# Where a transposed order is made: in TensorE's moving operand, or where ACT and DVE take the results over

## The chip, the cores and the metric

One NeuronCore of one Trainium2 chip. The metric is the device time of one execution in microseconds; the median of three runs of the kernel before is 582.38 us (581.98 to 582.94).

## The reference

An encoder layer on 512 tokens of 1024 channels, all float32. The tokens form a grid of 8 rows by 64 columns.

```python
h = rms_norm(x, g_pre) * (1.0 + scl) + shift
xa, za, q, k, v, zb, ga, gb = split(h @ w_in)          # each 512 x 1024
y_a = (rg_lru(conv(xa), forward) + rg_lru(conv(xa), backward)) * silu(za)
y_a = y_a @ w_pa
y_b = neighbourhood_attention(q, k, v, rpb) * silu(zb)  # 16 heads of 64, 8 rows x 16 columns of keys
y_b = y_b @ w_pb
merged = sigmoid(ga) * y_a + sigmoid(gb) * y_b
out = rms_norm(x + gate * (merged @ w_o), g_final)
```

## The kernel before

All activations are kept transposed: channels on the partitions, the 512 tokens along the free axis. A projection (`proj`) makes 128 output channels: it runs over eight blocks of 128 input channels, and for each issues three matmuls (`mm3`) of 128 x 128 weights against 128 x 512 tokens, since every float32 operand is split into a high and a low part of type fp32r (`whi` and `wlo` for weights, `hh`/`hl` or `hhl` for h, `ybhl` for y_b). That is 24 matmuls into one PSUM bank of the class `acc`.

The attention works on blocks of columns: the 64 columns of the grid are four blocks of 16, and all queries of one block (8 rows x 16 columns, 128 queries) share one window of 24 or 32 columns of keys. It therefore wants q, and everything that comes out of it, in the order *block, row, column*, while h, k and all of the rest are in the order of the tokens, *row, block, column*. In the kernel before the order is changed by TensorE as it reads its moving operand. The view `tok` takes 16 floats, hops 64 floats to the next row, and starts again 16 floats on for the next block:

```python
tok = lambda t: t.rearrange("p (r b c) -> p b r c", b=4, c=16)
nat = lambda t: t.rearrange("p (b r c) -> p r b c", b=4, c=16)
hhq, hlq = ([(d[k], lambda t=d[k]: tok(t.ap)) for k in range(KD)] for d in (hh, hl))
```

The projections of q and of zb (called z, the gate of the attention) read h through `tok`, so their results come out in block order. The projection of y_b with `w_pb` reads `ybhl`, which is in block order, through `nat` (16 floats, hop of 128), so its result comes out in token order. All other projections read plain tiles.

The main part runs in this order. First v is made (PSUM class `hx`), then eight rounds for eight pairs of heads: `proj` for q, k and z, and `attention(pr, q, k, z, ...)`. Then four groups of eight projections: two xa (`conv_gates`, with small matmuls into `gt`), two za (`gate_a`), two gates (`gate_m`), two of y_b with `w_pb`; then gates and `w_pa` in turn, and last the product with `w_o`.

In `attention`, ACT makes `qh` (L686) and `kh`, DVE the remainders `ql` (L687) and `kl` (helper, L339); the scale -1/8 is applied to q. Scores (`sp`) are twelve matmuls for two blocks; DVE adds the bias and takes the minimum (L717), ACT makes the exponential (L723), TensorE transposes (`pt`, L732), ACT and DVE split the result (`pp`, L737 and L739), TensorE multiplies with v (`pv`), ACT and DVE add the parts into `yt` (L754 to L760). The sums' reciprocals are spread (`rcx`, L775) and transposed into a bank `rcb` (L780, tile class `mi`); DVE multiplies the gate `sz` by 0.5 and by it (`szr`, L782), then `yt` by `sz` (`yb`, L784), and ACT and DVE split the product into `ybhl` (L336, L339).

The order of instructions on every engine is set by a planner (`Plan`) that simulates costs and ranks, so an attention's scores, transposes and products with v are interleaved with the projections that follow: the second half of a pair's attention lies beside the q and k of the next pair, and the eighth pair's beside the first xa projections. Weight tiles are cast by ACT (`whi`, L336) and split by DVE or POOL (`wlo`, L339); their loads are issued by SP and held back by the progress of TensorE (`gate_of`).

Of the kernel before, what the change touches and what calls it, by code (L numbers as in the profile page):

```python
# [8 lines left out]
F32 = mybir.dt.float32  # L9
F32R = mybir.dt.float32r  # L10
AF = mybir.ActivationFunctionType
ALU = mybir.AluOpType

P = 128
S = 512
D = 1024
KD = D // P
# [51 lines left out]
class Plan:  # L69
# [18 lines left out]
    def op(self, eng, cost, fn, rank, r=(), w=(), rw=(), lock=False, after=(), spare=0, size=0, until=None, name=""):  # L88
        o = Op()
        o.alts = {eng: cost} if isinstance(eng, str) else dict(zip(eng, cost))  # L90
        o.fn, o.rank, o.lock, o.spare, o.size, o.name = fn, rank, lock, spare, size, name
        o.n, o.until = len(self.ops), until
        deps = set()
        for t in list(r) + list(rw):
            for f in t.family():
                deps.update(f.writers)
        for t in list(w) + list(rw):
            for f in t.family():
                deps.update(f.readers)
        for t in r:  # L100
            t.readers.append(o)
        for t in w:
            t.writers.append(o)
        for t in rw:
            for f in [t] + t.parts:
                f.writers, f.readers = [], []
            t.writers = [o]
        o.tiles = list(dict.fromkeys(t.base or t for t in list(w) + list(rw) + list(r)))
        for t in o.tiles:
            t.uses += 1  # L110
        o.data, o.succ, o.t = set(deps), [], 0.0
        deps.update(after)
        o.left = len(deps)
        for d in deps:
            d.succ.append(o)
        self.ops.append(o)
        return o
# [155 lines left out]
def act(n, ptr=0, acc=False):  # L273
    return 0.19 + 0.833e-3 * n + 0.093 * ptr + 0.19 * acc


def dve(n):
    return 0.153 + 1.043e-3 * n
# [6 lines left out]
def pool_(n):  # L285
    return 0.17 + 2.33e-3 * n


def pe(n, passes=1):
    return passes * max(n / 2400.0 + 0.0135, 0.111)  # L290
# [3 lines left out]
def layer(ctx, tc, x, par, w_m, w_g, bc_gate, w_v, w_in, w_blk, rpb, amask, w_pa, w_pb, w_o, g_final, out):  # L294
    nc = tc.nc
# [6 lines left out]
    op = pl.op  # L302
# [6 lines left out]
    def T(name, dt=F32):  # L309
        return pl.tile("s", lambda i: sb.tile([P, S], dt, tag=f"s{i}", name=nm(name)))  # L310

    def W(name, dt=F32):
        return pl.tile("w", lambda i: sb.tile([P, D], dt, tag=f"w{i}", name=nm(name)))

    def two(name):

        t = W(name, F32R)
        return t.part(0, S), t.part(S, D)

    def B(cls):  # L320
        return pl.tile(cls, lambda i: ps.tile([P, 512], F32, tag=f"b{i}", name=nm(cls)))
# [7 lines left out]
    def load(t, dst, src, rank, size, after=(), spare=0, r=(), name="load"):  # L329

        return op("SP", 0.45, lambda e: nc.sync.dma_start(dst(), src() if callable(src) else src), rank,  # L331
                  r=r, w=[t], after=after, spare=spare, size=size, name=name)

    def cast(o, i):

        return lambda e: nc.scalar.copy(o(), i()) if e == "ACT" else nc.vector.tensor_copy(o(), i())  # L336

    def sub(o, a, b):
        return lambda e: ENGINE[e].tensor_tensor(o(), a(), b().bitcast(F32), op=ALU.subtract)  # L339
# [4 lines left out]
    def mm3(o, lh, ll, rh, rl, first, last):  # L344
        mm(o, lh, rh, first, False)
        mm(o, lh, rl, False, False)
        mm(o, ll, rh, False, last)

    def whole(t):
        return lambda: t.ap  # L350


    def const(name, shape, dt=F32):
# [14 lines left out]
       r=[par_sb, ident], w=[pp0])  # L368
# [62 lines left out]
    for t in range(NT):  # L431
# [7 lines left out]
        if t % 2:  # L439
            rstd_ops(2, [qap[i], qdp[i]], lambda i=i: (qa.ap[:, 2 * i:2 * i + 2], qd.ap[:, 2 * i:2 * i + 2]), -16.8 + 2 * i, rx[i])  # L440
            for h in range(2):
                for u in (t - 1, t):
                    def scale(e, u=u, h=h, i=i):
# [6 lines left out]
                       lock=True)  # L450
# [27 lines left out]
    hh, hl = {}, {}  # L478
# [134 lines left out]
    def gate_of(n, back):  # L613
        return [main[max(0, n - back)]] if n - back >= 0 else []

    def proj(w, rh, rl, lo="DVE"):

        n = len(main)
        raw, hi, low = W("wraw"), W("whi", F32R), W("wlo", F32R)
        v = lambda t: (lambda: t.ap.rearrange("p (k c) -> p k c", k=KD))  # L620
        load(raw, whole(raw), w, n - 5, 524288, after=gate_of(n, 5), spare=1,
             name=f"w{n}")
        op("ACT", act(1024), cast(whole(hi), whole(raw)), n - 2.2, r=[raw], w=[hi], after=gate_of(n, 3), name=f"whi{n}")
        engs = (lo,) if isinstance(lo, str) else lo
        costs = [dve(1024) if e == "DVE" else pool_(1024) for e in engs]
        op(engs, costs, sub(whole(low), whole(raw), whole(hi)), n - 2.1, r=[raw, hi], w=[low], lock=True, name=f"wlo{n}")
        o = B("acc")
        for k in range(KD):
            def f(e, k=k):
                mm3(o.ap, v(hi)()[:, k, :], v(low)()[:, k, :], rh[k][1](), rl[k][1](), k == 0, k == KD - 1)  # L630
            first = op("PE", pe(512, 3), f, 1000 + n + 0.01 * k, r=[hi, low, rh[k][0], rl[k][0]], rw=[o], name=f"p{n}")
            if k == 0:
                main.append(first)
        return n, o
# [2 lines left out]
    H = (slice(0, 64), slice(64, 128))  # L637

    tok = lambda t: t.rearrange("p (r b c) -> p b r c", b=4, c=16)
    nat = lambda t: t.rearrange("p (b r c) -> p r b c", b=4, c=16)  # L640
    hhl, hll = ([(d[k], whole(d[k])) for k in range(KD)] for d in (hh, hl))
    hhq, hlq = ([(d[k], lambda t=d[k]: tok(t.ap)) for k in range(KD)] for d in (hh, hl))

    def bias(pr, rank, after):
        raw = T("braw")
# [33 lines left out]
    ybh, ybl = {}, {}  # L679

    def attention(pr, q, k, z, nbt, pos):

        nq, oq = q
        nk_, ok = k
        qh, ql, kh, kl = (T(n, F32R) for n in ("qh", "ql", "kh", "kl"))
        op("ACT", act(512), lambda e: nc.scalar.activation(qh.ap, oq.ap, AF.Copy, scale=-0.125), nq - 1.9, r=[oq], w=[qh], name="qh")  # L686
        op("DVE", dve(512), lambda e: nc.vector.scalar_tensor_tensor(ql.ap, oq.ap, -0.125, qh.ap.bitcast(F32), op0=ALU.mult,  # L687
           op1=ALU.subtract), nq - 1.9, r=[oq, qh], w=[ql], name="ql")
        op("ACT", act(512), cast(whole(kh), whole(ok)), nk_ - 1.9, r=[ok], w=[kh], name="kh")
        op("DVE", dve(512), sub(whole(kl), whole(ok), whole(kh)), nk_ - 1.9, r=[ok, kh], w=[kl], name="kl")  # L690
        sm, yt = C("sm", 8), T("yt")
        off = (pr % 2) * 256
        def half(b0):
# [73 lines left out]
        sz, rc, rcb = T("sz"), C("rc", 8), B("mi")  # L767
# [4 lines left out]


        rx_ = T("rcx")
        op("ACT", act(512), lambda e: nc.scalar.copy(rx_.ap.rearrange("p (b c) -> p b c", b=8),  # L775
           rc.ap.unsqueeze(2).to_broadcast([P, 8, 64])), pos - 0.3, r=[rc], w=[rx_], name="rcx")

        def f(e_):
            for b in range(4):
                nc.tensor.transpose(rcb.ap[:, b * P:(b + 1) * P], rx_.ap[:, b * P:(b + 1) * P], ident.ap)  # L780
        op("PE", 0.47, f, pos - 0.3, r=[rx_, ident], w=[rcb], name="rcb")
        op("DVE", dve(512), lambda e: nc.vector.scalar_tensor_tensor(sz.ap, sz.ap, 0.5, rcb.ap, op0=ALU.mult, op1=ALU.mult),  # L782
           pos - 0.3, r=[rcb], rw=[sz], name="szr")
        op("DVE", dve(512), lambda e: nc.vector.tensor_tensor(yt.ap, yt.ap, sz.ap, op=ALU.mult), pos + 0.5, r=[sz], rw=[yt],  # L784
           lock=True, name="yb")
        ybh[pr], ybl[pr] = two("ybhl")
        op("ACT", act(512), cast(whole(ybh[pr]), whole(yt)), pos + 0.6, r=[yt], w=[ybh[pr]], name="ybh")
        op("DVE", dve(512), sub(whole(ybl[pr]), whole(yt), whole(ybh[pr])), pos + 0.6, r=[yt, ybh[pr]], w=[ybl[pr]], lock=True,
           name="ybl")

    def small(rank, after):
# [32 lines left out]
    LO_A = ("POOL",)  # L824
    att = []
    for pr in range(8):
        n0 = len(main)
        nbt = bias(pr, n0, gate_of(n0, 2) if pr else [main[6]])
        if pr % 2 == 0:
            load_v(pr // 2, gate_of(n0, 2) if pr else [])  # L830
        q = proj(w_in[16 + pr], hhq, hlq, LO_A if pr else "DVE")
        k = proj(w_in[24 + pr], hhl, hll, LO_A)
        z = proj(w_in[32 + pr], hhq, hlq, LO_A)
        attention(pr, q, k, z, nbt, k[0] + 0.6)


# [112 lines left out]
    for g in range(4):  # L949
        tiles = (2 * g, 2 * g + 1)  # L950
        n0 = len(main)
        ybv = lambda: ([(ybh[k], lambda t=ybh[k]: nat(t.ap)) for k in range(KD)], [(ybl[k], lambda t=ybl[k]: nat(t.ap)) for k in range(KD)])
        load_gates(g, n0, gate_of(n0, 3))
        for i in tiles:
            conv_gates(i, proj(w_in[i], hhl, hll))
        for i in tiles:
            gate_a(i, proj(w_in[8 + i], hhl, hll))
        recur(tiles, n0 + 10)
        for i in tiles:
            gate_m((i, 0), proj(w_in[48 + i], hhl, hll))  # L960
        for i in tiles:
            prod_m((i, 0), proj(w_pb[i], *ybv()), None)
# [128 lines left out]
    pos = [B("acc") for _ in range(NT)]  # L1091
# [8 lines left out]
    for t in range(NT):  # L1100
        for h in range(1 + (t == NT - 1)):
            w = 256 if t == NT - 1 else 512
# [87 lines left out]
```

## Time and profile before

| | |
|---|---|
| median of three runs | 582.38 us |
| the profiled execution | 582.45 us |
| its span | 580.5 us |
| DVE, ACT, POOL busy | 70%, 58%, 16% of the span |
| chain that ended last | PE 92%, DMA 4%, DVE 1%, ACT 1% |
| granted clock, mean | 0.996 |

The profiled execution is longer than its span by 1.95 us, which lie around the program. Busy shares say how much of the span an engine worked in, not whether anyone waited for it; the chain that ended last and the waits say that. L numbers are lines of the kernel before. A matmul's own duration in the trace includes the time in which the next one already runs, so the time that a matmul takes from TensorE is read from the distance between starts.

### The profile page before, as it was taken

Reading aid. Unit: us, or ns where it says so; the run is one execution under the profiler, and the core shown is the slowest. Engines: PE = TensorE matmul, PEld = TensorE weight load, DVE = VectorE, ACT = ScalarE, POOL = GpSimd, SP = SyncE. Lnnn points to the kernel's source line nnn. Section 1 sums busy time; section 2 is a strip of 40 time slices with the busy share of each in tenths; the row PEclk is TensorE's granted clock in tenths of the full one; section 3 lists DMA queues with packets and bytes.
Section 4 is the critical chain, followed back from the end, with each engine's and each line's share of the span. In section 5 each row is a group of like instructions: output and inputs, shape, how many; then the busy total and the mean of one; then the engine's idle time right before and its main releaser. Section 6 shows DMA issues by size and latency. Waiting matters only on the chain.

```text
span 580.5 us, 7725 instructions
## 1 busy us (share of the span) xinstructions
PE 570.9 (98%) x2829; PEld 465.5 (80%) x2829; DVE 403.8 (70%) x690; ACT 337.1 (58%) x584; POOL 92.6 (16%) x82
## 2 busy tenths in 40 slices
PE   8999999999999999999999999999999999999994
PEld 6878878878788788887887787788788888888884
DVE  5997966776776767777469639748947996365444
ACT  5765536546557465469957974993895333242132
POOL 0005427264372561000000000000000000000010
PEclk9999999999999999999999999999999999999998
DMA  7993988434335231222232133133129713380002
GB/s 275 411 403 96 349 254 260 134 103 153 94 114 175 57 100 62 73 73 96 103 111 91 38 107 129 36 110 108 64 87 331 272 46 108 112 321 2 0 37 109
DMA packets 30814, 81.34 MB, mean 140 GB/s; under 512 B 3264, under 2 KB 6456, under 8 KB 30777
## 3 DMA queue, kind: packets, MB, share of 16 engines
q1 hardware_dynamic: 30777, 80.86, 41.7%
q8 instruction: 22, 0.36, 0.3%
q14 instruction: 15, 0.12, 0.1%
HBM read 74.56 MB, written 6.29 MB: 139 GB/s over the span
## 4 chain that ended last, share of the span: by engine, by line
PE 92%; DMA 4%; DVE 1%; ACT 1%; issue 1%; SPq 0%; ACTq 0%
PE acc L342 76%; PE hx L342 6%; PE pv L342 3%; PE pt L732 3%; PE sp L342 2%; DMA wc<-in_w_m_dram 2%; PE gt L342 2%; DMA wv<-in_w_v_dram 2%; PE mi L780 1%; SPq L331 0%; ACT xr L1064 0%; DVE yo L1056 0%; DVE yo L1054 0%; DVE q L412 0%; PE mi L342 0%
## 5 line engine op out<-in xcount | busy, mean ns | idle before, releaser
L342 PE MATMUL acc<-hhl,whi 128*128 128x512 f32 x784 | 249.6, 400 | 0.0
L342 PEld LDWEIGHTS acc<-hhl,whi 128*128 128x128 f32 x784 | 141.8, 188 | 30.3 <-issue 2.9
L342 PE MATMUL acc<-hhl,wlo 128*128 128x512 f32 x392 | 154.1, 393 | 0.0
L342 PEld LDWEIGHTS acc<-hhl,wlo 128*128 128x128 f32 x392 | 73.8, 188 | 16.8
L336 ACT CAST whi<-wraw 128x1024 fp32r<-128x1024 f32 x72 | 74.1, 1046 | 3.7 <-DMA wraw<-in_w_in_dram 2.6
L339 DVE TENSOR_TENSOR wlo<-wraw,whi 128x1024 fp32r<-128x1024 f32 x49 | 59.2, 1220 | 11.9 <-ACT whi L336 11.2
L339 POOL TENSOR_TENSOR wlo<-wraw,whi 128x1024 fp32r<-128x1024 f32 x23 | 55.2, 2400 | 76.6 <-ACT whi L336 60.8
L1066 POOL TENSOR_TENSOR yo<-yo,gfin 128x512 f32<-128x512 f32 x4 | 5.2, 1288 | 345.6 <-ACT xr L1064 345.6
L723 ACT ACTIVATE p<-p,mn 128x192 f32<-128x192 f32 (+1 forms) x64 | 30.4, 477 | 30.0 <-DVE mn L717 30.0
L946 DVE SCALAR_TENSOR_TENSOR gm<-gm,acc 128x512 f32<-128x512 f32 x16 | 11.0, 688 | 43.0 <-PE acc L342 43.0
L661 POOL TENSOR_TENSOR nb<-msk,braw 128x192 f32<-128x192 f32 (+1 forms) x48 | 32.0, 698 | 55.1 <-DMA braw<-in_rpb_dram 55.1
L342 PE MATMUL acc<-woh,mhl 128*128 128x512 f32 (+1 forms) x144 | 40.4, 365 | 0.0
L342 PE MATMUL acc<-ybhl,whi 128*128 128x512 f32 x128 | 39.9, 392 | 0.0
L342 PE MATMUL acc<-yahl,whi 128*128 128x512 f32 x128 | 39.4, 389 | 0.0
L717 DVE CUSTOM_DVE_ANT_0 p<-sp,nb 128x192 f32<-128x192 f32 (+1 forms) x64 | 31.4, 592 | 9.5 <-PE sp L342 9.5
L342 PE MATMUL hx<-vh,hhl 128*128 128x512 f32 x112 | 35.4, 391 | 0.3 <-ACT hhl L336 0.3
L739 DVE TENSOR_TENSOR pp<-pt,pp 96x512 fp32r<-96x512 f32 (+1 forms) x32 | 22.0, 688 | 12.3 <-ACT pp L737 12.3
L342 PEld LDWEIGHTS acc<-woh,mhl 128*128 128x128 f32 x144 | 26.1, 189 | 4.4
L342 PEld LDWEIGHTS acc<-ybhl,whi 128*128 128x128 f32 x128 | 24.1, 188 | 5.7
L342 PEld LDWEIGHTS acc<-yahl,whi 128*128 128x128 f32 x128 | 24.0, 188 | 5.0
L342 PE MATMUL acc<-wol,mhl 128*128 128x512 f32 (+1 forms) x72 | 26.3, 365 | 0.0
L757 DVE TENSOR_TENSOR vp<-pv,vp 64x256 f32<-64x256 f32 x32 | 13.5, 421 | 18.0 <-ACT vp L754 17.5
(183 smaller groups left out, 1005.3 us busy)
## 6 DMA issues: line engine op xcount, KB each, us to landing
wraw<-in_w_in_dram SPq DMA_DIRECT2D x56, 512.0 KB
wc<-in_w_m_dram SPq DMA_DIRECT2D x16, 512.0 KB
vscr<-va SPq DMA_DIRECT2D x8, 512.0 KB
vt<-vscr SPq DMA_DIRECT2D x16, 256.0 KB
wraw<-in_w_pb_dram SPq DMA_DIRECT2D x8, 512.0 KB
wraw<-in_w_pa_dram SPq DMA_DIRECT2D x8, 512.0 KB
wr<-in_w_g_dram SPq DMA_DIRECT2D x16, 256.0 KB
wo<-in_w_o_dram SPq DMA_DIRECT2D x8, 512.0 KB
```

Of the source, the lines that this page charges most:

```text
L336: return lambda e: nc.scalar.copy(o(), i()) if e == "ACT" else nc.vector.tensor_copy(o(), i())
L339: return lambda e: ENGINE[e].tensor_tensor(o(), a(), b().bitcast(F32), op=ALU.subtract)
L342: nc.tensor.matmul(o, a, b, start=first, stop=last)
L661: nc.gpsimd.tensor_tensor(o, mv, view, op=ALU.subtract)
L717: nc.vector.tensor_tensor_reduce(out=o, in0=v(spv(h, e)[:, :nk]), in1=v(hv(nb)[:, h, :nk]), scale=1.0, scalar=3e38, op0=ALU.add, op1=ALU.m ...
L723: nc.scalar.activation(hv(pt_)[:, h, :nk], hv(pt_)[:, h, :nk], AF.Exp, bias=mn.ap[:, h:h + 1], scale=-1.0, accum_out=sm.ap[:, 2 * b + h:2 ...
L732: nc.tensor.transpose(pv4()[:4 * w, h, j, :], hv(pt_)[:, h, j * 4 * w:(j + 1) * 4 * w], ident.ap)
L739: op("DVE", dve(512), lambda e_, w=w, ppv=ppv, pv4=pv4: nc.vector.tensor_tensor(ppv()[:4 * w, :, :, 1, :], pv4()[:4 * w], ppv()[:4 * w, :, ...
L757: op("DVE", dve(256), lambda e_, h=h: nc.vector.tensor_tensor(v3()[H[h]], p3(pv[h])[H[h], :, 1, :], v3()[H[h]], op=ALU.add), rk - 0.45, r= ...
L780: nc.tensor.transpose(rcb.ap[:, b * P:(b + 1) * P], rx_.ap[:, b * P:(b + 1) * P], ident.ap)
L946: op("DVE", dve(512), lambda e: nc.vector.scalar_tensor_tensor(t.ap, t.ap, 1.0, o.ap, op0=ALU.add, op1=ALU.mult), n - 1.9, r=[o], rw=[t], ...
L1066: op(("DVE", "POOL"), (dve(w), pool_(w)), lambda e: ENGINE[e].tensor_tensor(y(), y(), gfin[n].ap[:, gs], op=ALU.mult), rank + 0.1, r=[gfin ...
```

## The change

TensorE reads h and y in the order of memory everywhere. q and z come out of their projections in token order. `qh` and `ql` read the PSUM bank of q through `tok` and write block order; since these two no longer carry the scale -1/8, `kh` and `kl` do. z stays in token order, so `sz` does; `szr` and `yb` read the reciprocals' bank and `yt` through `nat`, and `yb` writes into `sz`, which `ybhl` is split from, in token order. The factor 0.5 moves from `szr` to `rcx`.

```diff
+    brc = lambda t: t.rearrange("p (b r c) -> p b r c", b=4, c=16)
+    rbc = lambda t: t.rearrange("p (r b c) -> p r b c", b=4, c=16)
-    hhq, hlq = ([(d[k], lambda t=d[k]: tok(t.ap)) for k in range(KD)] for d in (hh, hl))
...
-        op("ACT", act(512), lambda e: nc.scalar.activation(qh.ap, oq.ap, AF.Copy, scale=-0.125), nq - 1.9, r=[oq], w=[qh], name="qh")
-        op("DVE", dve(512), lambda e: nc.vector.scalar_tensor_tensor(ql.ap, oq.ap, -0.125, qh.ap.bitcast(F32), op0=ALU.mult,
-           op1=ALU.subtract), nq - 1.9, r=[oq, qh], w=[ql], name="ql")
-        op("ACT", act(512), cast(whole(kh), whole(ok)), nk_ - 1.9, r=[ok], w=[kh], name="kh")
-        op("DVE", dve(512), sub(whole(kl), whole(ok), whole(kh)), nk_ - 1.9, r=[ok, kh], w=[kl], name="kl")
+        op("ACT", act(512), cast(lambda: brc(qh.ap), lambda: tok(oq.ap)), nq - 1.9, r=[oq], w=[qh], name="qh")
+        op("DVE", dve(512), sub(lambda: brc(ql.ap), lambda: tok(oq.ap), lambda: brc(qh.ap)), nq - 1.9, r=[oq, qh], w=[ql], name="ql")
+        op("ACT", act(512), lambda e: nc.scalar.activation(kh.ap, ok.ap, AF.Copy, scale=-0.125), nk_ - 1.9, r=[ok], w=[kh], name="kh")
+        op("DVE", dve(512), lambda e: nc.vector.scalar_tensor_tensor(kl.ap, ok.ap, -0.125, kh.ap.bitcast(F32), op0=ALU.mult,
+           op1=ALU.subtract), nk_ - 1.9, r=[ok, kh], w=[kl], name="kl")
...
-        op("ACT", act(512), lambda e: nc.scalar.copy(rx_.ap.rearrange("p (b c) -> p b c", b=8),
-           rc.ap.unsqueeze(2).to_broadcast([P, 8, 64])), pos - 0.3, r=[rc], w=[rx_], name="rcx")
+        op("ACT", act(512), lambda e: nc.scalar.activation(rx_.ap.rearrange("p (b c) -> p b c", b=8),
+           rc.ap.unsqueeze(2).to_broadcast([P, 8, 64]), AF.Copy, scale=0.5), pos - 0.3, r=[rc], w=[rx_], name="rcx")
...
-        op("DVE", dve(512), lambda e: nc.vector.scalar_tensor_tensor(sz.ap, sz.ap, 0.5, rcb.ap, op0=ALU.mult, op1=ALU.mult),
+        op("DVE", dve(512), lambda e: nc.vector.tensor_tensor(rbc(sz.ap), rbc(sz.ap), nat(rcb.ap), op=ALU.mult),
            pos - 0.3, r=[rcb], rw=[sz], name="szr")
-        op("DVE", dve(512), lambda e: nc.vector.tensor_tensor(yt.ap, yt.ap, sz.ap, op=ALU.mult), pos + 0.5, r=[sz], rw=[yt],
-           lock=True, name="yb")
+        op("DVE", dve(512), lambda e: nc.vector.tensor_tensor(rbc(sz.ap), nat(yt.ap), rbc(sz.ap), op=ALU.mult), pos + 0.5, r=[yt],
+           rw=[sz], lock=True, name="yb")
...
-        op("ACT", act(512), cast(whole(ybh[pr]), whole(yt)), pos + 0.6, r=[yt], w=[ybh[pr]], name="ybh")
-        op("DVE", dve(512), sub(whole(ybl[pr]), whole(yt), whole(ybh[pr])), pos + 0.6, r=[yt, ybh[pr]], w=[ybl[pr]], lock=True,
+        op("ACT", act(512), cast(whole(ybh[pr]), whole(sz)), pos + 0.6, r=[sz], w=[ybh[pr]], name="ybh")
+        op("DVE", dve(512), sub(whole(ybl[pr]), whole(sz), whole(ybh[pr])), pos + 0.6, r=[sz, ybh[pr]], w=[ybl[pr]], lock=True,
            name="ybl")
...
-        q = proj(w_in[16 + pr], hhq, hlq, LO_A if pr else "DVE")
+        q = proj(w_in[16 + pr], hhl, hll, LO_A if pr else "DVE")
         k = proj(w_in[24 + pr], hhl, hll, LO_A)
-        z = proj(w_in[32 + pr], hhq, hlq, LO_A)
+        z = proj(w_in[32 + pr], hhl, hll, LO_A)
...
-        ybv = lambda: ([(ybh[k], lambda t=ybh[k]: nat(t.ap)) for k in range(KD)], [(ybl[k], lambda t=ybl[k]: nat(t.ap)) for k in range(KD)])
+        ybv = lambda: ([(ybh[k], whole(ybh[k])) for k in range(KD)], [(ybl[k], whole(ybl[k])) for k in range(KD)])
```

The planner's costs and ranks are the same, and no instruction changes its place on any engine. What changes in place is seen on DVE beside the second q and k; this is the order before (`sz_890`, `yt_1004` and `ybhl_1105` belong to the first pair, `ql_1015` and `kl_1103` to the second, `acc` and `mi` are PSUM banks):

```order
L687 SCALAR_TENSOR_TENSOR ql_1015<-acc_882,qh_1001 128x512
L760 TENSOR_TENSOR yt_1004<-pv_945,vp_978 64x256
L782 SCALAR_TENSOR_TENSOR sz_890<-sz_890,mi_1006 128x512
L739 TENSOR_TENSOR pp_1011<-pt_980,pp_1011 96x4x128
L757 TENSOR_TENSOR vp_1065<-pv_1033,vp_1065 64x256
L757 TENSOR_TENSOR vp_1065<-pv_1034,vp_1065 64x256
L760 TENSOR_TENSOR yt_1004<-pv_1033,vp_1065 64x256
L760 TENSOR_TENSOR yt_1004<-pv_1034,vp_1065 64x256
L784 TENSOR_TENSOR yt_1004<-yt_1004,sz_890 128x512
L339 TENSOR_TENSOR kl_1103<-acc_994,kh_1096 128x512
L339 TENSOR_TENSOR ybhl_1105<-yt_1004,ybhl_1105 128x512
```

and this the order of the changed kernel at the same place (its lines are one further down):

```order
L339 TENSOR_TENSOR ql_1015<-acc_882,qh_1001 128x512
L761 TENSOR_TENSOR yt_1004<-pv_945,vp_978 64x256
L783 TENSOR_TENSOR sz_890<-sz_890,mi_1006 128x512
L740 TENSOR_TENSOR pp_1011<-pt_980,pp_1011 96x4x128
L758 TENSOR_TENSOR vp_1065<-pv_1033,vp_1065 64x256
L758 TENSOR_TENSOR vp_1065<-pv_1034,vp_1065 64x256
L761 TENSOR_TENSOR yt_1004<-pv_1033,vp_1065 64x256
L761 TENSOR_TENSOR yt_1004<-pv_1034,vp_1065 64x256
L785 TENSOR_TENSOR sz_890<-yt_1004,sz_890 128x512
L690 SCALAR_TENSOR_TENSOR kl_1103<-acc_994,kh_1096 128x512
L339 TENSOR_TENSOR ybhl_1105<-sz_890,ybhl_1105 128x512
```

The rows stand in the same places. `ql` and `szr` lose their scalar, `kl` gains one, and the product is now kept in `sz`.

## Rows read from the trace of the kernel before

**Rows 1.** Totals of the page: busy us, share of the span, instructions.

```profile
PE 570.9 (98%) x2829; PEld 465.5 (80%) x2829; DVE 403.8 (70%) x690; ACT 337.1 (58%) x584; POOL 92.6 (16%) x82
```

**Rows 2.** Waits of PE, whole span: us in total, times, longest.

```profile
PE mi L457 <- POOL onesc L360: 1.5, 1, 1.5
PE hx L342 <- ACT hhl L336: 0.3, 1, 0.3
```

**Rows 3.** Windows of PE: length, PE busy (instructions), granted clock, DMA share, GB/s.

```profile
65.51:71.25 5.74, 5.74 (x26) 1.00 1.02 374
71.25:76.74 5.49, 5.49 (x26) 1.00 0.92 274
99.90:106.72 6.82, 6.82 (x38) 1.00 0.30 106
222.55:231.98 9.43, 9.43 (x62) 1.00 0.18 57
245.73:254.93 9.20, 9.20 (x61) 1.00 0.18 60
281.88:287.32 5.44, 5.44 (x25) 1.00 0.27 96
287.32:292.89 5.57, 5.57 (x26) 1.00 0.30 94
292.89:298.44 5.55, 5.55 (x26) 1.00 0.27 94
```

**Rows 4.** Timeline of PE, a z; then behind gate matmuls: start, duration, operation.

```profile
99.90 0.40 PE L342 MATMUL acc<-hh,whi 128*128 128x512 f32 x1
...
103.25 0.41 PE L342 MATMUL acc<-hhl,wlo 128*128 128x512 f32 x1
103.59 0.35 PE L342 MATMUL sp<-kh,qh 64*128 64x192 f32 x2
...
105.05 0.40 PE L342 MATMUL acc<-hhl,wlo 128*128 128x512 f32 x1
...
106.72 0.41 PE L342 MATMUL acc<-hh,whi 128*128 128x512 f32 x1
...
264.88 0.39 PE L342 MATMUL acc<-hhl,wlo 128*128 128x512 f32 x1
...
266.48 0.62 PE L342 MATMUL acc<-hhl,whi 128*128 128x512 f32 x2
```

**Rows 5.** Groups by line and form, DVE: busy us, mean ns; idle before.

```profile
L717 DVE CUSTOM_DVE_ANT_0 p<-sp,nb 128x256 f32<-128x256 f32 x32 | 18.4, 656 | 2.6 <-PE sp L342 2.6
...
L717 DVE CUSTOM_DVE_ANT_0 p<-sp,nb 128x192 f32<-128x192 f32 x32 | 15.7, 529 | 6.9 <-PE sp L342 6.9
...
L687 DVE SCALAR_TENSOR_TENSOR ql<-acc,qh 128x512 fp32r<-128x512 f32 x8 | 5.5, 691 | 4.2 <-ACT qh L686 4.2
...
L599 DVE TENSOR_TENSOR va<-hx,va 128x512 fp32r<-128x512 f32 x8 | 5.4, 689 | 3.3 <-ACT va L598 3.3
```

**Rows 6.** Timelines of ACT, DVE and PE, second half of an attention.

```profile
116.34 0.60 ACT L686 ACTIVATE qh<-acc 128x512 fp32r<-128x512 f32 x1 [0.37 <-PE acc L342]
...
116.98 0.69 DVE L687 SCALAR_TENSOR_TENSOR ql<-acc,qh 128x512 fp32r<-128x512 f32 x1 [0.68 <-ACT qh L686]
...
118.16 0.69 DVE L782 SCALAR_TENSOR_TENSOR sz<-sz,mi 128x512 f32<-128x512 f32 x1
118.76 0.68 DVE L739 TENSOR_TENSOR pp<-pt,pp 96x512 fp32r<-96x512 f32 x1
...
120.52 0.64 PE L342 MATMUL pv<-pp,vt 96*128 96x256 f32 x4
```

**Rows 7.** Timeline of DVE ahead of the scores of 103.59.

```profile
101.10 0.69 DVE L339 TENSOR_TENSOR kl<-acc,kh 128x512 fp32r<-128x512 f32 x1
```

**Rows 8.** Timelines of DVE and PE: a split of weights and its projection.

```profile
417.55 1.22 DVE L339 TENSOR_TENSOR wlo<-wraw,whi 128x1024 fp32r<-128x1024 f32 x1
...
424.08 0.39 PE L342 MATMUL acc<-hh,whi 128*128 128x512 f32 x1
```

## The prediction

> **What bounds the kernel now.** I read the page's totals first: TensorE (PE) is busy for 570.9 of 580.5 us [rows 1]. A busy PE can still be one that matmuls fill badly, so the waits of PE come next: in the whole run it stands still for another engine twice, for 1.5 and 0.3 us, both in the prologue [rows 2]. From 65 us on nothing that ACT, DVE, POOL or a DMA does is ever waited for. So the time is the sum of what PE's instructions take one after another, and an edit counts if it makes those shorter, or if it makes another engine so late that PE begins to wait.
>
> The third view sets projections of 24 matmuls side by side, in stretches from the first matmul of one to the first of the next [rows 3]. A gate's projection, whose moving operand lies in order, takes 5.44 us: 24 x 226.7 ns. The two after it read y through `nat` and take 5.57 and 5.55 us. The very first q, read through `tok`, takes 5.74 us, and the k behind it, with h in order, 5.49 us. [...] Inside the attention stage the stretches hold scores and transposes too, but one pair can still be compared: the q of the eighth pair is interleaved with the attention of the seventh (9.43 us), and the first xa projection stands in the same place behind the eighth, with h in order (9.20 us). So the view alone is what costs: 0.30 us on a q without company (5.74 to 5.44), 0.23 us on one with it, and 0.12 us on a y.
>
> The fourth view is PE's order of time around one z. Its first 14 spacings take 3.35 us, 239.3 ns each; then come the scores; after them seven spacings from 105.05 to 106.72 take 1.67 us, 238.6 ns each. Behind the gate matmuls, contiguous ones at the same distance from small matmuls take 1.60 us for seven, 228.6 ns each [rows 4].
>
> **The change part by part.**
>
> *h read in order by q and z.* 16 projections, 384 matmuls. Seven q in company, whose stretches repeat to 0.01 us, save 0.23 us each, 1.61 us; the first q saves 0.30 us. A z saves 14 x (239.3 - 226.7) = 0.176 us ahead of its scores and 7 x (238.6 - 228.6) = 0.07 us behind them, 0.25 us; eight of them 2.00 us. Bounds for a z: not less than a y saves, 0.12 us; not more than 24 x 12.6 ns = 0.30 us. I take 0.25 because both its halves are worked out from rows of a z itself.
>
> *y read in order by w_pb.* 8 projections, 192 matmuls: four pairs save 0.13 + 0.11 us, 0.96 us. The projection behind each pair also sheds a little, some 0.02 us each, 0.08 us as an estimate from the k that follows q and takes 5.49 instead of 5.44 us.
>
> Sum: 1.61 + 0.30 + 2.00 + 0.96 + 0.08 = 4.95 us, all on PE and so all on the path.
>
> *The order made at the take-over.* `qh` (ACT) and `ql` (DVE) now read q's PSUM bank in runs of 16 floats; `szr` reads the reciprocals' bank, and `yb` reads yt, in such runs. The scale -1/8 goes from q to k and the 0.5 from `szr` to `rcx`, so forms change in place; no row of any engine's order moves and no DMA is added or moved, so nothing is passed on SP or POOL. No row of before shows a 16-float run on ACT or DVE. The nearest is the subtraction at L599, which writes runs of 64: 689 ns for 512 elements, against 691 for the `ql` of before with everything contiguous [rows 5]. Far off is L717, which writes single floats 32 bytes apart: from 192 to 256 elements it grows by 127 ns, 1.98 ns per element, where `ql` takes 1.35 per element all in [rows 5]. I take no extra cost, because a run of 16 is nearer to a run of 64 than to single floats; the other end is kept as a rival below. [...]
>
> Cover, if they do cost more: `qh`, `ql`, `szr` and the subtraction of the fourth probability block follow each other on ACT and DVE; that subtraction begins at 118.76, takes 0.68 us, and PE uses its result at 120.52, so 1.08 us are free [rows 6]. Behind `qh` on ACT stands the cast of the same block. `yb` is ahead of `kl` on DVE; `kl` ends at 101.79, and the scores that read it begin at 103.59 [rows 7, 4], 1.80 us later. `kh` and `kl` get the forms that `qh` and `ql` had, and those take 0.60 and 0.69 us against `kl`'s own 0.69 [rows 5, 6, 7]: nothing.
>
> *Does a faster PE run into something?* The distances above shrink by what PE gains within them: a z's 15 matmuls ahead of the scores, under 0.2 us of 1.80. Weights come early: counted in order of time, the tightest split is DVE's of 417.55; it ends at 418.77, and the projection that it belongs to begins at 424.08 and reads it from its third matmul on [rows 8]. The loads are issued against PE's own progress, so they move with it. The whole gain of 5 us is spread over 375 us and should meet no wait.
>
> 582.45 us of the profiled execution (span 580.5 and 1.95 around it) less 4.95 is 577.50; from the median of the runs shown, 582.38, it is 577.43. I predict **577.5 us**.
>
> **The rivals.**
>
> *Weaker in company (12%).* The rates of 227 and 239 ns are those of quiet stretches; behind scores and transposes contiguous matmuls may be slow too. If all 24 projections save only what a y saves: 24 x 0.12 = 2.9 us, **579.5 us**. The 0.23 of the eighth q speaks against it.
>
> *The view costs nothing (5%).* The extra time would then be DVE's and POOL's traffic beside q, z and y, and the change would not do what it says: **582.4 us**. For it: contiguous matmuls too are off 226.7 at times, as the 228.6 behind the gates show [rows 4]. Against it: first q and first k have the same small work beside them, 5.74 and 5.49 us. [...]
>
> *The take-over turns into a wait (slower, 4%).* If 16-float runs double `qh`, `ql` and `szr`, the fourth probability block is late by 0.60 + 0.69 + 0.69 = 1.98 us, 1.08 of it free, and PE stands 0.90 us ahead of the last product with v, in each of the seven places where a q lies beside an attention: 6.3 us lost, 4.95 won, **583.8 us**. It decides from 1.08 + 4.95/7 = 1.79 us for the three together. At L717's slope, 0.63 ns per element more or 0.32 us each, they need 0.97 us and still fit. Another 3% is for a price in between that eats part of the gain (578 to 582 us).
>
> **How the numbers follow.** The forecast has 76%: its own range goes from 576.6 (12.6 ns on all 384 q and z matmuls, 4.84 us, and 1.04 for y) to 578.5 (a y's 0.12 us on z alone). The weaker case, at 579.5, belongs inside; with the runs' own spread of about 0.5 us the range is **576.2 to 579.9 us**, and what is left out is the last three cases, 12%, and some misjudged size. A measurement of this kernel tells about 0.2% (1.2 us) from no change. Faster by more than that: forecast, weaker case and the price in between, 91%. Within it: the free view, 5%. Slower: 4%.
>
> **What would show it.** Right: first q and k both near 5.44 us, w_pb at 5.44, the eighth q at 9.20, z at 6.57 (6.82 less 0.25) [rows 3]; `qh`, `ql`, `szr` and `yb` with the durations that they had; PE's list of waits as short as now. Wrong: q stretches still at 9.43 us (the view is free); the product with v waiting on DVE (the take-over); `qh` or `ql` over 0.9 us; or z stretches that shrink by 0.1 us only (company).

## The result, and the profile after

The changed kernel takes 577.73 us (median of six runs, 577.39 to 578.03), the kernel before 581.99 us (median of six, 581.79 to 582.94). The ratio is 0.9924 with a 95% interval from 0.9914 to 0.9935: 3.8 to 5.0 us less, 4.26 us between the medians. 577.5 us was predicted.

The page's totals of the changed kernel, which answer to [rows 1], and its list of PE's waits, which answers to [rows 2]:

```profile
PE 566.2 (98%) x2829; PEld 465.1 (81%) x2829; DVE 404.4 (70%) x690; ACT 337.1 (59%) x584; POOL 91.7 (16%) x82
```

```profile
PE mi L457 <- POOL onesc L360: 1.5, 1, 1.5
```

PE's busy time fell by 4.7 us; ACT's stayed and DVE's rose by 0.6 us. No wait came in. The windows of PE, in the order first q, first k, a z, the eighth q, the first xa, a gate, two y (length, PE busy, clock, DMA share, GB/s; to be laid beside [rows 3]):

```profile
65.00:70.44 5.44, 5.44 (x26) 1.00 1.03 369
70.44:75.88 5.44, 5.44 (x26) 1.00 0.89 291
98.65:105.25 6.60, 6.60 (x38) 1.00 0.69 237
219.13:228.40 9.27, 9.27 (x61) 1.00 0.18 58
241.88:251.05 9.17, 9.17 (x61) 1.00 0.20 60
278.01:283.44 5.43, 5.43 (x25) 1.00 0.28 97
283.44:288.88 5.44, 5.44 (x25) 1.00 0.31 96
288.88:294.32 5.44, 5.44 (x25) 1.00 0.30 96
```

The five of these with nothing small beside them take 5.43 to 5.44 us, whatever they read. The granted clock is 1.00 as before. The eighth q fell from 9.43 to 9.27 us and not to 9.20, and a z from 6.82 to 6.60, where 6.57 was expected.

To leave the prologue out, I measure on PE's timeline from the first matmul of the first q to the first of the two half blocks that end the product with `w_o`: from 65.51 to 566.76 us before, which is 501.25 us, and 496.84 us now: 4.41 us less. (In the timeline of before the row of that last start is merged with the one ahead of it; 566.76 is put between the rows at 566.53 and 566.87, one spacing of 226.7 ns behind the first.) By kind of projection:

| | predicted, us | measured, us |
|---|---|---|
| first q | 0.30 | 0.30 |
| seven q in company | 1.61 | 1.17 |
| eight z | 2.00 | 1.74 |
| eight y | 0.96 | 0.92 |
| behind y (xa, ga); first xa, behind the last z | 0.08; none | 0.12 + 0.03 |
| k behind a q (the first; seven more) | none | 0.05 + 0.08 |
| sum | 4.95 | 4.41 |

The profiled span itself is 4.8 us shorter, since the first q also begins 0.5 us earlier. That is no effect of the change: in the executions of all kernels below the first q begins between 64.4 and 66.0 us, with the same code ahead of it.

The instructions that now make the order, in the groups by line and form of the changed kernel (mean ns behind the busy time), answer to [rows 5]:

```profile
L785 DVE TENSOR_TENSOR sz<-yt,sz 128x512 f32<-128x512 f32 x8 | 7.7, 960 | 0.3
...
L339 DVE TENSOR_TENSOR ql<-acc,qh 128x512 fp32r<-128x512 f32 x8 | 5.5, 691 | 3.7 <-ACT qh L336 3.7
...
L783 DVE TENSOR_TENSOR sz<-sz,mi 128x512 f32<-128x512 f32 x8 | 5.5, 688 | 0.2
```

```profile
L336 ACT CAST qh<-acc 128x512 fp32r<-128x512 f32 x8 | 4.7, 587 | 3.7 <-PE acc L342 3.7
```

`ql` took 691 ns contiguous and takes 691 in runs of 16 floats. `qh` as a cast in runs takes 587 ns, as the contiguous cast `kh` did from PSUM in the kernel before (L336, 587 ns).

### The profile page after: what moved, and what is told of

It is laid out like the page before. It is cut to its first block, busy times and chain, and to the rows that moved or that the text cites. A ratio compares the mean times of both kernels' runs of the same rounds, so it can differ in the third digit from the quotient of the medians.

```text
span 575.7 us, 7726 instructions
## 1 busy us (share of the span) xinstructions
PE 566.2 (98%) x2829; PEld 465.1 (81%) x2829; DVE 404.4 (70%) x690; ACT 337.1 (59%) x584; POOL 91.7 (16%) x82
## 4 chain that ended last, share of the span: by engine, by line
PE 97%; DVE 1%; ACT 0%; issue 0%; POOL 0%; POOLq 0%; ACTq 0%
PE acc L342 76%; PE hx L342 8%; PE pv L342 3%; PE pt L733 3%; PE sp L342 2%; PE gt L342 2%; PE mi L457 2%; PE hx L386 1%; PE hx L471 1%; PE mi L781 1%; ACT xr L1065 0%; DVE yo L1057 0%; DVE yo L1055 0%; DVE q L412 0%; PE mi L342 0%
## 5 line engine op out<-in xcount | busy, mean ns | idle before, releaser
L336 ACT CAST whi<-wraw 128x1024 fp32r<-128x1024 f32 x72 | 74.2, 1046 | 3.4 <-DMA wraw<-in_w_in_dram 2.6
```

## Experiments

**Each half alone.** The first kernel has q and z in order and leaves y in block order; the second is the opposite.

```diff
 # h_in_order: the changed kernel, but
-  tensor_tensor(rbc(sz.ap), rbc(sz.ap), nat(rcb.ap), op=mult)
+  tensor_tensor(brc(sz2.ap), tok(sz.ap), brc(rcb.ap), op=mult)
-  tensor_tensor(rbc(sz.ap), nat(yt.ap), rbc(sz.ap), op=mult)
+  tensor_tensor(yt.ap, yt.ap, sz2.ap, op=mult)
-  ybv: whole(ybh[k]), whole(ybl[k])
+  ybv: nat(ybh[k].ap), nat(ybl[k].ap)
```

> Half of the change: q and z read h in order and qh, ql and szr make the block order; y stays in block order and w_pb reads it through nat as before. My theory (the price is that of the hopping read, whichever projection pays it, and the parts add): 4.26 us of the whole change less the 0.96 to 1.0 us of y, so 3.3 us under the kernel before, ratio 0.9943; first q 5.44 us, a w_pb projection still 5.55 to 5.57 us. Rival (the gain is one effect of the whole, for instance of what the other engines do to TensorE): either the full 4.3 us or hardly any.

```diff
 # y_in_order: the kernel before, but
-  tensor_tensor(yt.ap, yt.ap, sz.ap, op=mult)
+  tensor_tensor(rbc(yn.ap), nat(yt.ap), nat(sz.ap), op=mult)
-  ybv: nat(ybh[k].ap), nat(ybl[k].ap)
+  ybv: whole(ybh[k]), whole(ybl[k])
```

> The other half: q and z read h through tok as before and the product yb is written in token order into a tile of its own, so that w_pb reads y in order. Theory: 0.96 to 1.04 us under the kernel before, ratio 0.998; first q 5.74 us, a w_pb projection 5.44 us. Rival (the view costs nothing): no difference, w_pb at 5.55 us.

h in order alone: 579.31 us against 582.58 of the kernel before beside it, ratio 0.9945 (0.9932 to 0.9958). y in order alone: 580.99 against 582.58, ratio 0.9975 (0.9966 to 0.9984). The product of the two is 0.9920, the whole change 0.9924. On PE, over the same stretch as above, they save 3.37 and 1.04 us, together 4.41, the whole to the last digit. First q and two y of the first kernel, by windows of PE:

```profile
64.42:69.85 5.43, 5.43 (x25) 1.00 1.01 375
282.86:288.42 5.56, 5.56 (x25) 1.00 0.31 94
288.42:293.97 5.55, 5.55 (x25) 1.00 0.27 94
```

and of the second:

```profile
65.44:71.17 5.73, 5.73 (x25) 1.00 1.03 374
287.25:292.69 5.44, 5.44 (x26) 1.00 0.32 96
292.69:298.13 5.44, 5.44 (x26) 1.00 0.30 96
```

Each projection pays for its own view; beside that, only the one right behind it pays a little (0.03 us behind a y, 0.05 us for the first k). That also settles the rival by which the view costs nothing.

**The take-over without its views.**

```diff
-  qh: cast(brc(qh.ap), tok(oq.ap))
+  qh: cast(whole(qh), whole(oq))
-  ql: sub(brc(ql.ap), tok(oq.ap), brc(qh.ap))
+  ql: sub(whole(ql), whole(oq), whole(qh))
-  tensor_tensor(rbc(sz.ap), rbc(sz.ap), nat(rcb.ap), op=mult)
+  tensor_tensor(sz.ap, sz.ap, rcb.ap, op=mult)
-  tensor_tensor(rbc(sz.ap), nat(yt.ap), rbc(sz.ap), op=mult)
+  tensor_tensor(sz.ap, yt.ap, sz.ap, op=mult)
```

> The changed kernel with the views of qh, ql, szr and yb left out: all four read and write in the order of memory, so queries and gates are left in token order where the attention takes them as blocks (this reordering is what is left out). Theory (runs of 16 floats cost ACT and DVE nothing, or it is covered): the time of the changed kernel, 577.7 us within 0.5, qh 587 ns, ql 691 ns, szr 688 ns as there. Rival (the views cost something that ends up on TensorE's path): 0.5 to 1 us faster than the changed kernel, or shorter qh, ql or szr.

577.41 us, ratio to before 0.9913 (0.9899 to 0.9928); the changed kernel's 0.9924 lies inside. PE's stretch is 496.84 us in both. The groups of DVE:

```profile
L785 DVE TENSOR_TENSOR sz<-yt,sz 128x512 f32<-128x512 f32 x8 | 7.7, 961 | 0.3
L339 DVE TENSOR_TENSOR ql<-acc,qh 128x512 fp32r<-128x512 f32 x8 | 5.5, 691 | 3.7 <-ACT qh L336 3.7
L783 DVE TENSOR_TENSOR sz<-sz,mi 128x512 f32<-128x512 f32 x8 | 5.5, 689 | 0.3
```

961, 691 and 689 ns without views, 960, 691 and 688 with them: runs of 16 floats cost DVE nothing here, whether they are read from PSUM (`ql`, `szr`) or from SBUF (`yt`, by `yb`). `qh`, which ACT reads from PSUM in such runs, is at 587 ns with them and 588 without. The price was not covered, there was none.

**How much was covered.** `ql` is issued two and four times, which lengthens the chain by real DVE work.

```diff
-  op("DVE", dve(512), sub(...), nq - 1.9, r=[oq, qh], w=[ql], name="ql")
+  op("DVE", dve(512), lambda e: [sub(...)(e) for _ in range(N)], nq - 1.9, r=[oq, qh], w=[ql], name="ql")
```

> The changed kernel with the subtraction that makes ql issued twice, which puts 0.6 to 0.7 us more on DVE ahead of szr and of the fourth block's subtraction. Theory (1.1 us are free there, which is why a dearer take-over would not have cost anything at first): the time of the changed kernel, ratio to before 0.992 to 0.993; the q stretches still 9.26 us. Rival (the cover is used up or DVE's time counts directly): 7 x 0.6 = 4 us slower, ratio 0.9995.

> The same with ql issued four times, 1.9 to 2.0 us more on DVE. Theory: 1.1 us of it are free, the rest, 0.8 to 0.9 us, makes TensorE wait ahead of the last product with v in each of seven pairs: 6 us over the changed kernel, about 583.7 us, ratio to before 1.002 to 1.003; the k stretch behind the q longer by 0.8 us. Rival (the chain is not what I took it for): no loss, or the whole 7 x 2.0 = 14 us.

Twice: 577.88 us, ratio 0.9928 (0.9911 to 0.9945), as the changed kernel; the q stretches are 9.26 us and six of the seven k stretches behind them keep their time. The k of the eighth pair does not: 7.03 us against 6.90 in the changed kernel.

```profile
228.96:235.99 7.03, 7.03 (x38) 1.00 0.23 75
```

So 0.13 of the 0.7 us are lost there, and only about 0.6 us are free: behind that `ql` DVE makes two halves of `yt` ahead of `szr` (0.86 us), in the other places one (0.43 us). Four times: 586.88 us, ratio 1.008 (1.006 to 1.0101), 9.15 us above the changed kernel (9.0 above the kernel with `ql` twice, run beside it) where I had expected 6. PE's waits, and the place in the timeline of all engines, of that last kernel:

```profile
PE pv L342 <- DVE pp L740: 7.0, 7, 1.3
PE mi L457 <- POOL onesc L360: 1.5, 1, 1.5
PE sp L342 <- DVE kl L690: 0.3, 1, 0.3
```

```profile
118.10 2.87 DVE L339 TENSOR_TENSOR ql<-acc,qh 128x512 fp32r<-128x512 f32 x4 [0.60 <-ACT qh L336]
...
122.05 0.68 DVE L740 TENSOR_TENSOR pp<-pt,pp 96x512 fp32r<-96x512 f32 x1
...
122.78 0.53 PEld L342 LDWEIGHTS pv<-pp,vt 96*128 96x128 f32 x4 [1.38 <-DVE pp L740]
122.78 0.74 PE L342 MATMUL pv<-pp,vt 96*128 96x256 f32 x4 [0.95 <-DVE pp L740]
```

The mechanism and its seven places are as I had named them. Four subtractions take 2.87 us, 2.18 more than one (0.69) and not the 2.0 that I had put; the stretch of the k beside it grows from 6.92 us in the changed kernel to 8.14:

```profile
114.51:121.43 6.92, 6.92 (x37) 1.00 0.21 48
```

```profile
117.28:125.42 8.14, 7.19 (x38) 1.00 0.17 39
```

So 2.18 - 1.22 = 0.96 us of the chain are free, not the 1.08 that I had read between the end of the subtraction and PE's first use. The row of PEld (TensorE's weight loads) gives a reason: the load of v's weights waits for the subtraction too, though it reads none of it. Without the wait it begins 0.22 us ahead of its matmul (120.30 and 120.52 before), here only behind the wait, at 122.78. Six of the seven places lose 1.21 to 1.25 us, the k of the eighth pair, with less free, 1.56: 8.9 us. Another 0.5 us is lost once, in the first z, where the scores wait for `kl`.

**Was the first xa a fair picture of a q in order?**

```diff
-  conv_gates(i, proj(w_in[i], hhl, hll))
+  conv_gates(i, proj(w_in[i], *(seen if i == 0 else (hhl, hll))))   # seen: h through tok
```

> The changed kernel with the first xa projection, which stands beside the eighth pair's attention, reading h through tok (so the convolution of the first 128 channels gets its tokens in another order, a wrong result there). Theory (the stretch that I took as the picture of a q in order is not one, since its small matmuls stand elsewhere in it; the view costs 0.16 to 0.17 us in such company, as 9.43 to 9.26 us shows): 9.17 to 9.34 us. Rival (the first xa is a fair picture and q has lost something else on the way): 9.17 to 9.40 us.

The window of PE, 9.32 us against 9.17 in the changed kernel (one execution):

```profile
241.60:250.92 9.32, 9.32 (x62) 1.00 0.19 59
```

The view costs 0.15 us there, as the 0.16 to 0.17 of the q and not 0.23, so q lost nothing on the way. The xa stretch is 0.1 us shorter than a q's at equal views, in order and through `tok` alike. The order of PE gives a reason, which no run tests by itself: a q's 24 matmuls stand in six pieces (3, 6, 3, 6, 3, 3), the last of them behind the stretch's last transposes; the xa's stand in five (6, 6, 3, 6, 3), and it ends at the transposes themselves, so that one restart behind small matmuls falls to the next stretch. Behind transposes the first spacing of a piece is 0.31 to 0.32 us where the following ones are 0.22 to 0.24.

**Sixteen views.** All gate projections, which have nothing small beside them, read h through `t.rearrange("p (r b c) -> p b r c", b=b, c=c)` with various b and c, runs of c floats that hop by b x c. A second kernel exchanges the places of ga and gb. Each was executed once.

```diff
-  gate_m((i, 0), proj(w_in[48 + i], hhl, hll))
+  gate_m((i, 0), proj(w_in[48 + i], *seen(i)))       # view i
-  gate_m((i, 1), proj(w_in[40 + i], hhl, hll))
+  gate_m((i, 1), proj(w_in[40 + i], *seen(8 + i)))   # view 8 + i
```

> The changed kernel, in which the 16 gate projections (ga and gb) read h through 16 views, each of another length of run and another hop, so that their results come out in another order of tokens (wrong gates). Each stretch is 24 matmuls with nothing small between: 5.44 us in order. Runs x hop in floats: (16,32) (16,64 = tok) (16,128) (16,256) (32,64) (32,128) (64,128) (64,256) for gb; (16,128 = nat) (1,64) (8,64) (4,64) (2,64) (8,32) (4,32) (8,128) for ga. Theory (a price per hop that depends on the distance: 0.39 ns for 64 floats, 0.15 ns for 128): tok 5.74 us, nat and (16,128) both 5.56, (32,64) 5.59, (32,128) 5.50, (64,128) 5.47, (8,64) 6.03, (4,64) 6.6, (2,64) 7.8, (1,64) 10 us or more. [...] Rival 2 (the number of hops alone counts): tok and nat at the same price, all runs of 16 alike.

> The 16 views again with the places of ga and gb exchanged, so that each view is read by another projection, with other weights in another weight tile and other neighbours (wrong gates as there). Theory (the price belongs to the view alone): each view's stretch within 0.03 us of the other place: (16,32) 5.76, tok 5.74, (16,128) and nat 5.55, (16,256) 5.76, (32,64) 5.67, (32,128) 5.60, (64,128) and (64,256) 5.45, (8,64) 6.04, (4,64) 6.67, (2,64) and (1,64) 11.75, (8,32) and (8,128) 5.54, (4,32) 5.91. Rival (the price comes from meeting the weight loads in memory, and so depends on where the weights lie): differences of 0.1 us and more, the odd order of (16,128) and (16,256) gone.

The windows of the first kernel, in the order of the list in the expectation:

```profile
273.20:278.96 5.76, 5.76 (x25) 1.00 0.11 45
278.96:284.70 5.74, 5.74 (x25) 1.00 0.26 91
320.98:326.54 5.56, 5.56 (x26) 1.00 0.32 97
326.54:332.29 5.75, 5.75 (x25) 1.00 0.22 80
368.59:374.26 5.67, 5.67 (x25) 1.00 0.00 0
374.26:379.86 5.60, 5.60 (x25) 1.00 0.30 94
416.14:421.59 5.45, 5.45 (x25) 1.00 0.31 96
421.59:427.03 5.44, 5.44 (x25) 1.00 0.00 2
437.91:443.48 5.57, 5.57 (x26) 1.00 0.95 340
443.48:455.23 11.75, 11.75 (x25) 1.00 0.49 183
455.23:461.27 6.04, 6.04 (x26) 1.00 0.86 260
466.75:473.42 6.67, 6.67 (x25) 1.00 0.26 80
478.90:490.65 11.75, 11.75 (x25) 1.00 0.00 0
497.10:502.63 5.53, 5.53 (x25) 1.00 0.29 95
508.11:514.02 5.91, 5.91 (x26) 1.00 0.01 3
519.51:525.05 5.54, 5.54 (x26) 1.00 0.70 227
```

`tok` takes 5.74 us and `nat` 5.57 (its twin (16,128) 5.56), on h as on y and q: the price goes with the view. At a hop of 64 floats runs of 16, 8 and 4 cost 0.30, 0.60 and 1.23 us over 5.44, in each case 0.39 to 0.40 ns per hop (0.30 us / 24 matmuls / 32 hops, and so on), as I had expected. The rest of my theory falls: the distance does not set the price. Runs of 16 cost as much at hops of 32 and 256 as at 64 (5.76 and 5.75 us against 5.74), and only at 128 two fifths of it (0.12 us); runs of 8 are almost free at hops of 32 and 128 (0.09 and 0.10 us); and runs of 32 pay more per hop than runs of 16, 0.60 ns at 64 floats and 0.42 at 128. The rival of the number of hops alone falls with the same rows. At a hop of 64, runs of 4 floats take 6.67 us, and runs of 2 take as long as single floats, 11.75.

In the second kernel 12 of the views come within 0.03 us of these times, as expected, the odd order of (16,128) and (16,256) included; (1,64) and (8,32) come within 0.05. Two do not:

```profile
326.82:332.99 6.17, 6.17 (x26) 1.00 0.23 88
...
375.94:389.19 13.25, 13.25 (x26) 1.00 0.00 0
```

These are (8,64), 6.04 in the other place, and (2,64), 11.75. So the place has a part for these two, both of short runs, while the other short runs keep their times. What decides there stays open, and with it why the price depends on the hop as it does.

## Why the prediction was right, point by point

- *577.5 us.* Hit to 0.2 us, in part by luck: the gain of 4.95 us was 0.69 too large against the medians, and the six runs of the kernel before lie 0.46 us under the 582.45 from which it was taken.
- *PE sets the time, and no wait would come in.* Right: 4.41 us fewer on PE and 4.26 us fewer in the medians, and from the first q on PE still waits for nothing.
- *The view alone is what costs.* Right, shown by each half alone and by views put on projections that had none. What in the view costs, and why `nat` costs less than `tok`, is not shown.
- *First q 0.30 us, y 0.96 us.* Right: 0.30 and 0.92; what follows a y gained 0.12 instead of 0.08. The sum left out that the k behind a q and the xa behind the last z gain too (0.13 and 0.03 us), though the first k's 5.49 us was read.
- *Seven q at 0.23 us.* Too large: 0.17 each, 1.17 us in place of 1.61. Here the step that failed is "the first xa projection stands in the same place behind the eighth": it stands at the same time, but its stretch is cut at another point of the small matmuls. The kernel with the first xa through `tok` shows 0.15 us for the view in that company. Matmuls in order do not keep to 226.7 ns there: within the pieces of the eighth q they start 224 to 236 ns apart, those through `tok` 231 to 247.
- *Eight z at 0.25 us.* Somewhat large: 0.22 each. The 14 spacings ahead of the scores came out as worked: 98.65 to 101.83 in the timeline below is 227.1 ns each. The seven behind the scores, priced by matmuls behind the gates (1.60 us), take 1.63 (from 103.62 to 105.25): scores were dearer neighbours here than gate matmuls.

```profile
98.65 0.39 PE L342 MATMUL acc<-hh,whi 128*128 128x512 f32 x1
...
101.83 0.39 PE L342 MATMUL acc<-hhl,wlo 128*128 128x512 f32 x1
...
103.62 0.40 PE L342 MATMUL acc<-hhl,wlo 128*128 128x512 f32 x1
...
105.25 0.40 PE L342 MATMUL acc<-hh,whi 128*128 128x512 f32 x1
```

- *The take-over costs nothing.* Right, and by no cover: the durations are the same to 1 ns without the views.
- *The slower rival.* Its mechanism exists and its place was right, but it would have decided sooner, at about 0.96 + 4.41/7 = 1.59 us for the three instructions and not at 1.79, and sooner still by the eighth pair's k, where only some 0.6 us are free.
- *Weaker in company.* This rival had a part of the truth: q and z in company save 73 and 87% of what was put down for them, far from the half that it would have given.

## What to carry to other kernels

Where TensorE is the bound, look at the access pattern of its moving operand before anything else: here runs of 16 floats with hops cost it 0.12 to 0.30 us in every projection of 24 matmuls, while ACT and DVE made the same order once, as they took the result out of PSUM, and paid nothing for it (`qh` 587 ns against 588 contiguous, `ql` 691 with and without). Read the price of a view from two stretches with the same instructions between, and count the pieces into which small matmuls cut them before calling them equal. A gap between a producer's end and its consumer's start is not all slack: here 0.12 of 1.08 us could not be used.

## What was not expected of the hardware

- A hop of 64 floats cost a matmul's moving operand 0.39 to 0.40 ns, for runs of 16, 8 and 4 alike (in the other place 0.48 for runs of 8, 6.17 us), but 0.60 ns for runs of 32; at a hop of 128 floats runs of 16 cost 0.16 ns per hop, and runs of 8 at 32 and 128 floats 0.06 to 0.07. Runs of 64 were free (5.44 and 5.45 us).
- Runs of 2 floats were as slow as single floats: 11.75 us for 24 matmuls, 490 ns each against 226.7; in another place the same view took 13.25 us.
- ACT and DVE took PSUM banks over in runs of 16 floats at 587 and 691 ns, the times of contiguous reads (588 and 691).
